# Two-layer decoder: a layer's product triple of 272, 272, 272 columns becomes 274, 270, 272

## The chip, the core and the metric

One core of a Trainium2 chip runs the whole program. The metric is the device time in microseconds, a median of three runs; a profile of one more execution shows where it goes. Engines: TensorE (PE in the profile) multiplies matrices, VectorE (DVE) and ScalarE (ACT) work element by element, GpSimd (POOL) makes masks and small copies, SyncE (SP) issues most DMAs.

## What is computed

A decoder trunk of two layers over T = 272 tokens (16 learned meta tokens and 256 of input), width 2048, 16 heads. Layer 0 has softmax attention with forget gates, layer 1 stick-breaking attention on a shared K/V. Each layer has a squared-ReLU MLP of width 8192. Only the 256 input tokens are returned, so layer 1 works on 256 columns, but K/V is made from all 272. Cut to the main line:

```python
for layer in range(DEPTH):
    a = rms_norm(h, norm_attn[layer])
    if layer < N_A_LAYERS:
        q, k, v, f_logit = split(a @ fox_w_in[i])
        o = forgetting_attention(q, k, v, cum_logf)
        h = h + o @ fox_w_o[i]
    else:
        k_s, v_s = split(rms_norm(h, kv_norm) @ w_kv)
        o = stick_breaking_attention(a @ sb_w_q[i], k_s, v_s)
        h = h + o @ sb_w_o[i]
    h = h + squared_relu_mlp(rms_norm(h, norm_mlp[layer]), w_up[layer], w_down[layer])
return rms_norm(h, final_norm)[:, N_META:]
```

## The kernel before

Activations lie feature-major: 128 features on the partitions, 16 chunks of features, and the tokens as columns (272 in layer 0, 256 in layer 1). All large products keep fp32 accuracy by splitting: an operand is the sum of a high part, rounded to the type fp32r, and a low part, the rest. A product W·x is then three products of the fast type, accumulated in the same PSUM tile: W high by x high, W high by x low, W low by x high. Such a set of three is called a triple below.

`Split` (line 121) holds the two parts of an activation in one SBUF tile, 640 columns for each chunk: in layer 0 the high part at columns 48 to 319, the low part at 368 to 639 (`ROWS`, line 27), with free columns between them. In layer 1 it also gives `wide`, the high part with six zero columns behind it. The parts are written by ACT (high) and DVE (low) in `split_chunk` (line 137), in `put_split` for attention outputs (line 456) and in the MLP's evacuation (lines 640 and 641).

`gemm_group` (line 230) makes 512 output features, four results of 128 in four PSUM tiles (`accs`). It walks over four blocks `kb` of four chunks. `weights` (line 201) fetches a block by DMA in two halves on SP's queue and splits it, high on ACT (line 225), low on DVE (line 226); there are four buffers of raw and of split weights. In the first and last block the products go result by result (12 in a row for one result), in the two others by halves of the block. Layer 0 (`t0 = 0`) takes the three products of a triple one behind the other (line 258); layer 1 takes all high-by-high products of a run first, then the others (line 256). In every fourth group of layer 1 three products take `wide` and so 262 columns. Every product is issued in `gemm_matmul` (line 190), and so has line 192 in the profile; outside the first group it also ties each product behind the one before, so that their order stands as written. A scheduler decides where the attention's own products go between them, and the order of ACT and DVE.

After the last block each result is handed to `evac`, which the caller gives: q, k and v are scaled into SBUF (lines 468 and 472), out-projections add to the residual stream and split the next input (lines 616 to 620), MLP up-projections apply ReLU, square and split (lines 633 to 642), down-projections add to the residual (line 306). Groups with 272 columns: 12 for q, k and v of layer 0, 4 for its out-projection, 32 for its MLP (four chunks `f` of 2048 hidden features, each four groups up and four down), 8 for the shared K/V; 56 in all.

Of the kernel before, what the change touches and what calls it, by code (L numbers as in the profile page):

```python
# [9 lines left out]
F32 = mybir.dt.float32  # L10
F32R = mybir.dt.float32r
AF = mybir.ActivationFunctionType
ALU = mybir.AluOpType
AX = mybir.AxisListType

P = 128
# [4 lines left out]
T = M + S  # L21
# [12 lines left out]
def yoco_kernel(ctx: ExitStack, tc: tile.TileContext, hT_in, gains, b_f, w_f, w_qkv0, w_o0, w_up, w_dn,  # L34
                w_kv, w_q1, w_o1, g_row, out):
    nc = tc.nc
# [7 lines left out]
    tmp = ctx.enter_context(tc.tile_pool(name="tmp", bufs=2))  # L44
# [76 lines left out]
    class Split:  # L121


        def __init__(self, label, t0):
            n = T - t0
            self.t0 = t0
            rows = xs.tile([P, NC * XROW + 64], F32R, tag="x", name=f"x_{label}")
            hi, lo = ROWS[t0]
            rows = rows[:, hi:hi + NC * XROW].rearrange("p (c t) -> p c t", c=NC)
            d = lo - hi  # L130
            self.hi, self.lo = rows[:, :, :n], rows[:, :, d:d + n]
            if t0:

                self.wide = rows[:, :, :n + 6]
                nc.gpsimd.tensor_copy(rows[:, :, n:n + 6], pad[:, :6].unsqueeze(1).to_broadcast([P, NC, 6]))

    def split_chunk(sp, gi, c):

        g = g_sb[:, gi, c:c + 1]
        nc.scalar.activation(sp.hi[:, c], hT[:, c, sp.t0:], AF.Copy, scale=g)  # L140
        nc.vector.scalar_tensor_tensor(out=sp.lo[:, c], in0=hT[:, c, sp.t0:], scalar=g,
                                       in1=sp.hi[:, c].bitcast(F32), op0=ALU.mult, op1=ALU.subtract)

    class Norm:

# [84 lines left out]
    def gemm_group(wblk, sp, t0, evac, before={}, after={}, load_x=None):  # L230

        uid[0] += 1
        u = uid[0]
        accs = [pacc.tile([P, 512], F32, tag="acc", name=f"acc_{u}_{m}") for m in range(4)]
        n = T - t0
        for kb in range(4):
            if kb in before:
                before[kb]()  # L240
            parts, on_act, on_dve = weights(u, kb, wblk, 16 if t0 else 0, load_x)
            if kb in after:
                with tc.issue_after(on_act.ins), tc.issue_after(on_dve.ins):
                    after[kb]()

            if load_x is not None and kb == 0:
                runs = [([kc], range(4)) for kc in range(4)]
            elif kb in (0, 3):
                runs = [(range(4), [m]) for m in range(4)]
            else:  # L250
                runs = [(range(2 * hf, 2 * hf + 2), range(4)) for hf in range(2)]
            pinned[0] = load_x is None
            for kcs, ms in runs:
                pairs = ((0, sp.hi), (0, sp.lo), (1, sp.hi))
                if t0:
                    products = [(kc, m, *pair) for pair in pairs for kc in kcs for m in ms]
                else:
                    products = [(kc, m, *pair) for m in ms for kc in kcs for pair in pairs]
                left = {m: 3 * len(kcs) for m in ms}

                wide = [(0, 0, 0), (1, 0, 1), (2, 1, 1)] if t0 and u % 4 == 1 else []
                if u == 90:

                    wide = [(0, 0, 0), (0, 0, 1), (0, 2, 1)]
                for kc, m, part, x in products:
                    first, left[m] = kb == kc == 0 and left[m] == 3 * len(kcs), left[m] - 1
                    nw = n
                    if m == (0 if u == 90 else 3) and x is sp.hi and (kb, kc, part) in wide:
                        x, nw = sp.wide, n + 6
                    gemm_matmul(accs[m][:, :nw], parts[kc // 2][part][:, kc % 2, m * P:(m + 1) * P], x[:, 4 * kb + kc],  # L270
                                start=first, stop=kb == kc == 3 and left[m] == 0)
                if kb == 3:
                    for m in ms:
                        evac(m, accs[m][:, :n])

    def token_group(wblk, sp, done):
# [135 lines left out]
    def scratch(t, products):  # L412
        for pr in range(2):
            y = t[:, pr].rearrange("p (c x) -> p c x", c=4)
            for a in range(4):
                ins = nc.scalar.dma_start(v_dram[pr].rearrange("c j a x -> a j c x")[a], y[32 * a:32 * a + 32])
                behind(ins, products[pr])
# [38 lines left out]
    def put_split(sp, h, nh, t, n, src):  # L456
        hi, lo = (x[:, h:h + nh, t - sp.t0:t - sp.t0 + n] for x in (sp.hi, sp.lo))
        nc.scalar.activation(hi, src, AF.Copy)
        nc.vector.tensor_tensor(out=lo, in0=src, in1=hi.bitcast(F32), op=ALU.subtract)

    ao = Split("o0", 0)
    for g in range(4):
# [72 lines left out]
        for pr in range(2):  # L535
# [9 lines left out]
            for a in range(4):  # L545
# [10 lines left out]
                                in0=pm[:, P - M:P].unsqueeze(1).to_broadcast([P, 8, M]))  # L556
# [32 lines left out]
        def outputs(g=g, pps=pps, vT=vT, own=own, turned=turned):  # L589
            if turned is not None:  # L590
                scratch(turned, issued[20:60:20])
                vs = values_back(turned, issued[100:120:10], issued[160:180:10], f"0_{g}")
            for pr in range(2):
                raw, p0, p1 = pps[pr]

                p0 = p0.rearrange("p x i q -> p x (i q)").rearrange("p x (a h b i) -> p x h b a i", a=4, h=2, b=2)
                p0 = [[p0[:, k, i] for i in range(2)] for k in range(2)]
                p1 = p1.rearrange("p i q -> p (i q)").rearrange("p (a h i) -> p h a i", a=4, h=2)
                v0, v1 = vs[pr] if turned is not None else token_major(vT, pr, 0, f"0_{g}_{pr}")
                po = patt.tile([P, 2, 256], F32, tag="patt", name=f"po0_{g}_{pr}")  # L600
                for i in range(2):
                    weighted(po, v0, p0, i)
                    nc.tensor.matmul(po[:, i, P:], v1[:, i, :], p1[:, i], start=False, stop=i == 1)  # L603
                ends = po.rearrange("p i (c q) -> p (i c) q", c=2)[:, :, P - M:]
                nc.vector.tensor_tensor(out=ends, in0=ends, in1=own[:, 4 * pr:4 * pr + 4], op=ALU.add)
                put_split(ao, 4 * g + 2 * pr, 2, M, S, po)

        if g == 3:
            outputs()
# [14 lines left out]
    def mlp(layer, xm, norm, t0, last_evac, last_group=None):  # L624
        box = {}

        def get_rstd():
            box["r"] = norm.finish()

        for f in range(N_FF):  # L630
            u = Split(f"u{layer}_{f}", t0)
            for g in range(4):
                def evac(m, acc, g=g):
                    c = 4 * g + m
                    r = tmp.tile([P, T], F32, tag="relu", name=f"relu_{layer}_{f}_{c}")
                    u2 = tmp.tile([P, T], F32, tag="u2", name=f"u2_{layer}_{f}_{c}")
                    nc.vector.scalar_tensor_tensor(out=r[:, t0:], in0=acc, scalar=0.0, in1=box["r"][:, t0:],
                                                   op0=ALU.max, op1=ALU.mult)
                    nc.scalar.activation(u2[:, t0:], r[:, t0:], AF.Square)
                    nc.scalar.activation(u.hi[:, c], u2[:, t0:], AF.Copy)  # L640
                    nc.vector.tensor_tensor(out=u.lo[:, c], in0=u2[:, t0:], in1=u.hi[:, c].bitcast(F32),
                                            op=ALU.subtract)
                gemm_group(w_up[layer, f, g], xm, t0, evac, {2: get_rstd} if f == g == 0 else {})
                if last_group is not None and f == N_FF - 1 and g == 0:
                    to_token_major()
            for g in range(4):
                def evac(m, acc, g=g):
                    residual_add(4 * g + m, acc, t0)
                    if f == N_FF - 1:
                        last_evac(4 * g + m)  # L650
                if last_group is not None and f == N_FF - 1 and g == 3:
                    last_group(w_dn[layer, f, g], u)
                else:
                    gemm_group(w_dn[layer, f, g], u, t0, evac)
# [32 lines left out]
    ao = Split("o1", M)  # L687
    for g in range(4):
# [12 lines left out]
        kc = packed(kT[:, :, 240:T], f"kc_{g}")  # L701
# [23 lines left out]
        for pr in range(2):  # L725
# [10 lines left out]
            if pr == 0:  # L736
# [4 lines left out]
                                    in1=maskB[:, 0:256].unsqueeze(1).to_broadcast([P, 2, 256]))  # L741
            nc.vector.tensor_tensor(out=zp[:, :, 256:400], in0=pb[:, :, :144], op=ALU.add,
                                    in1=maskB[:, 256:400].unsqueeze(1).to_broadcast([P, 2, 144]))
# [20 lines left out]
            for t in (240, 384):  # L764
                nc.vector.tensor_tensor(out=zp[:, :, t:t + M], in0=zp[:, :, t:t + M],
                                        in1=sc[:, 2 * pr:2 * pr + 2, :], op=ALU.add)
# [184 lines left out]
```

## Time and profile before

| | |
|---|---|
| median of 3 runs | 2280.68 us (2280.51 to 2281.49) |
| the profiled execution, first to last instruction | 2278.5 us |
| PE busy | 2271.1 us, 18898 products |
| weight loads (PEld) | 2262.8 us |
| DVE busy, ACT busy | 1333.5 us, 1065.1 us |
| mean granted clock of TensorE | 0.999 |

The profile has one execution only, so sums are made against its 2278.5 us; the median of the timed runs is 2.2 us above that. How to read it: "mean ns" of a product is from its start to its modelled end, and products overlap, so it is not the time by which one product puts off the next. That time is the distance between starts, and in a stretch without waits it is the length of the stretch over the number of products. The chain of waits lists such stretches as pieces with a count.

### The profile page before, as it was taken

What the parts mean: (1) busy time and instruction counts of PE and PEld (TensorE: products, weight loads), DVE (VectorE), ACT (ScalarE), POOL (GpSimd) and SP (SyncE); (2) the same over time, 40 slices, a digit from 0 to 9 for tenths busy, and PEclk for the clock granted to TensorE, in tenths of its full rate; (3) what the DMA queues carried; (4) which work ended last, traced back from release to release, by engine and by line L of the source; (5) the groups of instructions that cost most, each with busy time, mean ns of one, the idle gap of its engine ahead of it and who ended that gap; (6) DMA issues with size and microseconds to landing.
All of it is one profiled execution on the core that took longest, in us unless ns stands there. A gap on an engine that the chain in (4) does not pass through costs nothing.

```text
span 2278.5 us, 44956 instructions
## 1 busy us (share of the span) xinstructions
PE 2271.1 (100%) x18898; PEld 2262.8 (99%) x18898; DVE 1333.5 (59%) x1930; ACT 1065.1 (47%) x1471; POOL 39.4 (2%) x72
## 2 busy tenths in 40 slices
PE   9999999999999999999999999999999999999998
PEld 9999999999999999999999999999999999999998
DVE  7767566554455455455566666666555555555555
ACT  6444445443354344335445555555443544543554
POOL 1000000000000000000000000000000000000001
PEclk9999999999999999999999999999999999999999
DMA  7765665555555555555556555555656556566564
GB/s 238 228 198 188 222 184 176 181 172 180 182 176 185 167 185 179 174 185 169 186 183 193 168 174 169 167 185 190 202 187 201 192 189 201 184 200 195 186 201 141
DMA packets 146171, 425.19 MB, mean 187 GB/s; under 512 B 31648, under 2 KB 43824, under 8 KB 145968
## 3 DMA queue, kind: packets, MB, share of 16 engines
q1 hardware_dynamic: 113760, 406.29, 54.1%
q10 hardware_dynamic: 32208, 16.02, 2.6%
q8 instruction: 148, 2.42, 0.4%
q14 instruction: 55, 0.45, 0.1%
HBM read 413.85 MB, written 8.41 MB: 185 GB/s over the span
## 4 chain that ended last, share of the span: by engine, by line
PE 99%; DMA 0%; issue 0%; POOL 0%; SPq 0%; POOLq 0%; ACT 0%; DVE 0%
PE acc L192 97%; PE po L435 0%; PE ps L435 0%; PE pza L435 0%; DMA raw<-w_qkv 0%; PE pzb L735 0%; PE po L804 0%; PE ps L508 0%; PE po L603 0%; PE pf L354 0%; PE pta L757 0%; PE pta L756 0%; PE pv L394 0%; POOL ob L850 0%; PE ptb L709 0%
## 5 line engine op out<-in xcount | busy, mean ns | idle before, releaser
L226 DVE TENSOR_TENSOR wlo<-raw,whi 128x1024 fp32r<-128x1024 f32 (+1 forms) x773 | 928.5, 1216 | 715.6 <-ACT whi L225 706.6
L225 ACT ACTIVATE whi<-raw 128x1024 fp32r<-128x1024 f32 (+1 forms) x773 | 796.4, 1050 | 961.0 <-PE acc L192 913.4
L192 PE MATMUL acc<-x_m,whi 128*128 128x272 f32 (+1 forms) x4096 | 643.1, 282 | 0.0
L192 PE MATMUL acc<-x_u,whi 128*128 128x272 f32 (+1 forms) x3968 | 626.0, 282 | 0.0
L192 PEld LDWEIGHTS acc<-x_m,whi 128*128 128x128 f32 x4096 | 566.0, 188 | 0.1
L192 PEld LDWEIGHTS acc<-x_u,whi 128*128 128x128 f32 x3968 | 550.4, 188 | 0.0
L192 PE MATMUL acc<-x_m,wlo 128*128 128x272 f32 (+1 forms) x2048 | 441.4, 282 | 0.0
L192 PE MATMUL acc<-x_u,wlo 128*128 128x272 f32 (+1 forms) x1984 | 432.1, 282 | 0.0
L192 PE MATMUL acc<-x_a,whi 128*128 128x272 f32 (+1 forms) x2048 | 355.4, 286 | 0.2 <-ACT whi L225 0.2
L192 PEld LDWEIGHTS acc<-x_m,wlo 128*128 128x128 f32 x2048 | 323.5, 188 | 0.0
L192 PEld LDWEIGHTS acc<-x_u,wlo 128*128 128x128 f32 x1984 | 315.3, 188 | 0.0
L192 PEld LDWEIGHTS acc<-x_a,whi 128*128 128x128 f32 x2048 | 301.3, 189 | 1.7 <-ACT whi L225 1.1
L192 PE MATMUL acc<-x_a,wlo 128*128 128x272 f32 (+1 forms) x1024 | 253.8, 286 | 0.0
L192 PE MATMUL acc<-x_kv,whi 128*128 128x272 f32 x1024 | 191.7, 288 | 0.0
L192 PEld LDWEIGHTS acc<-x_a,wlo 128*128 128x128 f32 x1024 | 175.7, 188 | 0.7 <-DVE ssq_a L158 0.4
L192 PE MATMUL acc<-x_o,whi 128*128 128x272 f32 (+1 forms) x1024 | 163.1, 283 | 0.0
L192 PEld LDWEIGHTS acc<-x_kv,whi 128*128 128x128 f32 x1024 | 160.1, 189 | 0.1
L192 PE MATMUL acc<-x_kv,wlo 128*128 128x272 f32 x512 | 147.6, 288 | 0.0
L192 PEld LDWEIGHTS acc<-x_o,whi 128*128 128x128 f32 x1024 | 142.3, 188 | 0.0
L307 DVE TENSOR_TENSOR hT<-acc,hT 128x272 f32<-128x272 f32 (+1 forms) x156 | 67.3, 431 | 75.4 <-PE acc L192 75.2
L192 PE MATMUL acc<-x_o,wlo 128*128 128x272 f32 (+1 forms) x512 | 110.7, 282 | 0.0
L192 PEld LDWEIGHTS acc<-x_kv,wlo 128*128 128x128 f32 x512 | 96.6, 189 | 0.0
(255 smaller groups left out, 1065.5 us busy)
## 6 DMA issues: line engine op xcount, KB each, us to landing
raw<-w_up SPq DMA_DIRECT2D x256, 512.0 KB, 3.9
raw<-w_dn SPq DMA_DIRECT2D x256, 512.0 KB, 4.0
raw<-w_qkv SPq DMA_DIRECT2D x92, 512.0 KB, 4.3
raw<-w_o SPq DMA_DIRECT2D x64, 512.0 KB, 3.9
raw<-w_kv SPq DMA_DIRECT2D x64, 512.0 KB, 4.4
raw<-w_q SPq DMA_DIRECT2D x32, 512.0 KB, 4.7
p_dram<-raw_p ACTq DMA_DIRECT2D x32, 96.0 KB, 4.6
v_dram<-turned ACTq DMA_DIRECT2D x48, 64.0 KB, 3.8
```

Source lines behind the costliest of these rows:

```text
L192: ins = nc.tensor.matmul(*args, **kw).ins
L225: on_act = nc.scalar.activation(hp, src, AF.Copy)
L226: on_dve = nc.vector.tensor_tensor(out=lp, in0=src, in1=hp.bitcast(F32), op=ALU.subtract)
L307: nc.vector.tensor_tensor(out=hT[:, c, t0:], in0=acc, in1=hT[:, c, t0:], op=ALU.add)
```

## The change

For activations of 272 columns, the high part's tile gets `more` further columns (2; 4 and 6 in the second and third chunk of the MLP) right behind it, in the free space of the row. `ended` copies the last `more` columns of the low part into them. The product of high weights with the high part now covers 272 + `more` columns, so its last columns are high weights by the last low columns; the product with the low part covers only 272 - `more`; the third stays at 272. The sums in the last columns of the PSUM tile belong to the columns `more` to the left of the tile's 272nd. Before each result is handed to `evac`, ACT copies them to SBUF (`rest`) and DVE adds them in place. In the changed kernel the lines from here on stand up to 22 lines lower.

```diff
     class Split:
-        def __init__(self, label, t0):
+        def __init__(self, label, t0, more=2):
             n = T - t0
-            self.t0 = t0
+            self.t0, self.more = t0, 0 if t0 else more
...
+            else:
+                self.wide, self.end = rows[:, :, :n + more], rows[:, :, n:n + more]
+                self.short = self.lo[:, :, :n - more]
+
+        def ended(self, c, nch=1):
+
+            if self.more:
+                nc.vector.tensor_copy(self.end[:, c:c + nch], self.lo[:, c:c + nch, T - self.more:])
 
     def split_chunk(sp, gi, c):
...
+        sp.ended(c)
...
                     nw = n
-                    if m == (0 if u == 90 else 3) and x is sp.hi and (kb, kc, part) in wide:
+                    if sp.more and x is sp.lo:
+                        x, nw = sp.short, n - sp.more
+                    elif sp.more and part == 0:
+                        x, nw = sp.wide, n + sp.more
+                    elif m == (0 if u == 90 else 3) and x is sp.hi and (kb, kc, part) in wide:
                         x, nw = sp.wide, n + 6
...
                     for m in ms:
+                        if sp.more:
+                            ends = accs[m][:, n - sp.more:n]
+                            rest = tmp.tile([P, 8], F32, tag="rest", bufs=4, name=f"rest_{u}_{m}")[:, :sp.more]
+                            nc.scalar.copy(rest, accs[m][:, n:n + sp.more])
+                            nc.vector.tensor_tensor(out=ends, in0=ends, in1=rest, op=ALU.add)
                         evac(m, accs[m][:, :n])
...
                 put_split(ao, 4 * g + 2 * pr, 2, M, S, po)
+                ao.ended(4 * g + 2 * pr, 2)
...
-            u = Split(f"u{layer}_{f}", t0)
+            u = Split(f"u{layer}_{f}", t0, (2, 4, 6, 2)[f])
...
+                    u.ended(c)
```

## The prediction

> **What bounds the kernel now.** I read the page first, then the longest pieces of the chain of waits in order of time, then the PE groups with shapes kept apart, then the PE timeline at a few places.
>
> ```profile
> span 2278.5 us, 44956 instructions
> ...
> PE 2271.1 (100%) x18898; PEld 2262.8 (99%) x18898; DVE 1333.5 (59%) x1930; ACT 1065.1 (47%) x1471; POOL 39.4 (2%) x72
> ...
> PEclk9999999999999999999999999999999999999999
> ...
> PE acc L192 97%; PE po L435 0%; PE ps L435 0%; PE pza L435 0%; DMA raw<-w_qkv 0%; PE pzb L735 0%; PE po L804 0%; PE ps L508 0%; PE po L603 0%; PE pf L354 0%; PE pta L757 0%; PE pta L756 0%; PE pv L394 0%; POOL ob L850 0%; PE ptb L709 0%
> ```
>
> TensorE is busy in all of the span, its clock is granted in full, and 97% of the chain is line 192, the projection products. Nothing else decides the end. What a product costs is read from how many follow one another in a stretch without a wait, not from its "mean ns", since products overlap. The two longest pieces of the chain, start, length and what:
>
> ```profile
> 427.93 756.83 PE acc L192 x6144
> ...
> 1581.78 533.37 PE acc L192 x4704
> ```
>
> The first lies in layer 0: 756.83 / 6144 = 123.2 ns for a product of 272 columns. The second lies in layer 1: 533.37 / 4704 = 113.4 ns for 256 columns. Sixteen columns more cost 9.8 ns, or 0.61 ns each, while 113.4 / 256 is 0.44 ns each. So 272 columns pay a surcharge. The PE timeline shows its form (start, length, engine, line); these are the products with wlo, the third of each triple, in layer 0:
>
> ```profile
> 600.07 0.29 PE L192 MATMUL acc<-x_u,wlo 128*128 128x272 f32 x1
> ...
> 600.43 0.29 PE L192 MATMUL acc<-x_u,wlo 128*128 128x272 f32 x1
> ...
> 600.81 0.28 PE L192 MATMUL acc<-x_u,wlo 128*128 128x272 f32 x1
> ...
> 601.17 0.29 PE L192 MATMUL acc<-x_u,wlo 128*128 128x272 f32 x1
> ...
> 601.55 0.29 PE L192 MATMUL acc<-x_u,wlo 128*128 128x272 f32 x1
> ```
>
> The triples take 0.36, 0.38, 0.36, 0.38 us in turn: equal work, two prices, alternating. In other stretches the same triple has another price:
>
> ```profile
> 143.15 0.29 PE L192 MATMUL acc<-x_a,wlo 128*128 128x272 f32 x1
> ...
> 143.53 0.29 PE L192 MATMUL acc<-x_a,wlo 128*128 128x272 f32 x1
> ...
> 143.91 0.29 PE L192 MATMUL acc<-x_a,wlo 128*128 128x272 f32 x1
> ```
>
> Here it is 0.38 each time. In layer 1 a stretch just before a product that the kernel widens to 262 columns is dearer than the one after it:
>
> ```profile
> 1583.50 1.11 PE L192 MATMUL acc<-x_m,wlo 128*128 128x256 f32 x8
> 1584.45 1.99 PE L192 MATMUL acc<-x_m,whi 128*128 128x256 f32 x16
> ...
> 1587.18 1.07 PE L192 MATMUL acc<-x_m,whi 128*128 128x256 f32 x8
> 1588.09 0.62 PE L192 MATMUL acc<-x_m,wlo 128*128 128x256 f32 x4
> 1588.54 1.07 PE L192 MATMUL acc<-x_m,whi 128*128 128x256 f32 x8
> ```
>
> From 1583.50 eight products take 0.95 us, 119 ns each; from 1587.18 twelve take 1.36 us, 113.3 ns each. So the cost of a product is not a function of its width alone: a stream of equal products locks into one of several rhythms and keeps it until something uneven passes. That is what the change touches.
>
> **A unit for the sum.** I count in steps of 113.33 / 17 = 6.67 ns, the time that 16 columns and no surcharge would take: 256 columns are 16 blocks of 16 and cost 17 steps, blocks plus one. 272 columns are 17 blocks; plus one would be 18 steps, 120.0 ns. They cost 123.2 to 123.3, which is 18.5: 18 and 19 in turn. A triple is then 18+19+18 = 55 steps (366.7 ns) or 19+18+19 = 56 (373.3), which are the 0.36 and 0.38 of the rows; the stretch at 143 us is at 57 (380).
>
> **The change, part by part.** *Widths.* In layer 0 and in the shared K/V projection each triple of 272, 272, 272 becomes 274, 270, 272 (276, 268, 272 in MLP chunk 1, and 278, 266, 272 in chunk 2). How many:
>
> ```profile
> L192 PE MATMUL acc<-x_m,wlo 128*128 128x272 f32 x1024 | 293.9, 287 | 0.0
> ...
> L192 PE MATMUL acc<-x_u,wlo 128*128 128x272 f32 x1024 | 293.9, 287 | 0.0
> ...
> L192 PE MATMUL acc<-x_a,wlo 128*128 128x272 f32 x768 | 216.9, 289 | 0.0
> ...
> L192 PE MATMUL acc<-x_kv,wlo 128*128 128x272 f32 x512 | 147.6, 288 | 0.0
> ...
> L192 PE MATMUL acc<-x_o,wlo 128*128 128x272 f32 x256 | 73.5, 287 | 0.0
> ```
>
> One wlo product per triple: 1024 + 1024 + 768 + 512 + 256 = 3584 triples. Columns stay at 816 in each. In blocks, 274 (and 276, 278) reaches into an 18th, while 270, 268 and 266 still need 17: 18 + 17 + 17 = 52, and one step more for each product gives 55. That is the cheaper of the two prices that alternate now. I take it that the uneven triple ends the alternation, as a wider product ends the dear stretch above. Then each pair of triples saves one step: 3584 / 2 x 6.67 = 11.9 us. The trace has no stream of uneven widths, so this is a choice between ends. The low end is 54 steps, each product at 18 as if the two columns beyond the block were free: 3584 x 1.5 x 6.67 = 35.8 us saved. For this end speaks the run with a 262-column product:
>
> ```profile
> 1749.04 1.08 PE L192 MATMUL acc<-x_m,whi 128*128 128x262 f32 x8
> 1749.95 0.62 PE L192 MATMUL acc<-x_m,wlo 128*128 128x256 f32 x4
> ```
>
> Its eight products take 0.91 us, as the eight from 1587.18 without it, so six columns past the block cost no more than about 0.01 us. The high end is 56.5 steps, the extra block paid and the alternation kept: one step more per triple, 23.9 us. I take 55, between them, since it is a price that 272-column triples already show.
>
> The Trainium skill ("TensorE: Matmul & The Clock Gate", section "Back-to-back issue gap") prices a warm product in isolation at N / 2.4 + 2.5 ns, a straight line in the columns. By it a triple would be 347.5 ns with either split, and the change would be worth nothing; the trace disagrees with the figure, at 123.2 ns for 272 columns against its 115.8, and with a straight line through one stream, since one width has several prices here.
>
> *Side work.* Each of 56 groups (12 for q, k and v, 4 out-projections, 32 MLP, 8 K/V) has 4 results, so 224 tiny copies on ACT (rest) and 224 adds on DVE; and 120 copies on DVE move the end columns of the low part (ended). Nearest rows, small copies and adds out of PSUM:
>
> ```profile
> L803 ACT COPY own<-pvc 128x64 f32<-128x64 f32 x4 | 0.8, 198 | 0.0
> ...
> L805 DVE TENSOR_TENSOR po<-po,own 128x32 f32<-128x32 f32 x8 | 1.6, 195 | 2.7 <-PE po L804 2.7
> ...
> L377 DVE COPY fq_sb<-pfq 128x32 f32<-128x32 f32 x1 | 0.2, 191 | 1.5 <-PE pfq L376 1.5
> ```
>
> ACT gets 224 x 0.20 = 45 us, DVE 344 x 0.19 = 65 us. Both have room: ACT is busy 47% and DVE 59%, and their largest waits are for PE and for each other (columns: us in total, times, longest):
>
> ```profile
> ACT whi L225 <- PE acc L192: 913.4, 466, 4.6
> ...
> DVE wlo L226 <- ACT whi L225: 706.6, 419, 3.6
> ```
>
> The new waits are: on ACT the copy waits for the last product of a result, with weight splits (line 225) queued behind it, which wait for PE anyway; on DVE the add waits for that copy, with the evacuation and a weight split behind it. An accumulator is wanted again only after the three other results' runs of 12 products, 3 x 12 x 0.123 = 4.4 us, and the addition delays it by 0.4. I cost it at nothing. Were that cover gone at each group, 56 x 0.4 = 22 us would be the price.
>
> *Order.* In the built program PE has the same products, and the order on the queues of SP and POOL and of the DMAs on ACT is unchanged. In MLP and out-projection the PE order is unchanged too; in the attention stages the scheduler lets attention products slide by up to 49 places and ACT and DVE instructions change places with neighbours. There the DMA that comes back from scratch is what can come late:
>
> ```profile
> ACT v L385 <- DMA turned<-v_dram: 6.6, 6, 2.7
> ```
>
> ACT waits 6.6 us in all for it now and PE hardly waits; I take 0 for the new order, with 6.6 us either way as bounds, which lie inside the range below.
>
> *The start.* The first product of a chunk now reads the copied low columns, so it waits for the low split too.
>
> ```profile
> 4.85 0.50 DVE L141 SCALAR_TENSOR_TENSOR x_a<-hT,g_sb,x_a 128x272 fp32r<-128x272 f32 x1
> ...
> 4.98 1.16 PE L192 MATMUL acc<-x_a,whi 128*128 128x272 f32 x5
> ...
> 7.23 1.26 PE L192 MATMUL acc<-x_a,whi 128*128 128x272 f32 x8 [0.22 <-ACT whi L225]
> ```
>
> The low split ends at 5.35; with 0.19 for the copy PE begins at about 5.55 instead of 4.98. Part of that 0.6 us is taken back in the wait at 7.23: 0 to 0.6, I take 0.5.
>
> **Sum.** 2278.5 - 11.9 + 0.5 = 2267.1 us of span. The median of the runs is 2280.7, 2.2 us above this span, and I keep that: **2269.3 us**.
>
> **Rivals.** *Every product at 18 steps or nearly* (54 to 54.5 per triple): the uneven triple lets each product find the cheap rhythm that 256 columns have. For it: the cheap run after the wide product and the free six columns. Against: no stretch of 272 is that cheap. 54.5 gives 3584 x 6.67 = 23.9 saved, 2257.3; 54 gives 2245.4.
>
> *Only columns count*: the sum stays 816 and the surcharge belongs to the load of columns, not to a rhythm. Against it: three prices for one width. Time 2280.7 + 0.5 = 2281.2.
>
> *The extra block* (the slower side): 274 columns pay a further step, 270 give none back, and the alternation goes on in part or in full. It decides from where the triple averages over 55.5 steps, 370 ns. For it: longer products show larger surcharges, not a constant one.
>
> ```profile
> 2257.03 1.99 PE L192 MATMUL acc<-whi,x_u 128*128 128x512 f32 x8
> ...
> 2259.78 1.99 PE L192 MATMUL acc<-whi,x_u 128*128 128x512 f32 x8
> ```
>
> Twelve products of 512 columns take 2.75 us, 229.2 ns or 34.4 steps each, 2.4 above their 32 blocks; and the 57-step stretch shows that worse rhythms exist. At 56 steps the loss is 11.9 us, 2293.1; at 56.5 it is 23.9, 2305.1.
>
> **How the numbers follow.** Forecast (55 steps) 0.37, cheaper rhythm 0.30, columns only 0.09, extra block 0.24. The measurement can tell about 0.2% from no change, 4.6 us. So faster 0.67, same 0.09, slower 0.24. The range runs from the cheap end, 2245, to just above the 56-step case, 2294; what it leaves out is the dearer half of the extra block and the cover's loss. If faster, the likeliest part is 2245 to 2271.
>
> **What would show each step right or wrong.** The long layer-0 piece of the chain: 122.2 ns per product if right, 120 to 121 for the cheaper rhythm, 123.2 if only columns count, 124.4 or more for the extra block. The distance between wlo products on the timeline: a steady 0.37 instead of 0.36 and 0.38. Layer 1's piece must stay at 113.4. The MLP chunks, with their own widths, would differ if the overhang matters and not the unevenness. A new wait of PE on "rest" or on the copied ends beyond the first 10 us would make the side work wrong, and so would weight splits that come late behind the new copies.

## The result and the profile after

The change makes the kernel slower: 2309.2 us against 2280.6 us before, a ratio of 1.0127 (95% interval 1.0113 to 1.0141). The profiled execution spans 2306.4 us, 27.9 more than before. From the page of the changed kernel: the span, and busy time, share and instructions of each engine.

```profile
span 2306.4 us, 45617 instructions
...
PE 2296.7 (100%) x18898; PEld 2287.5 (99%) x18898; DVE 1381.4 (60%) x2274; ACT 1092.9 (47%) x1695; POOL 21.6 (1%) x72
```

TensorE has the same 18898 products as before and is busy all the time, so its products follow one another more slowly. The two long pieces of the chain of waits (start, length, what) say where:

```profile
436.19 771.25 PE acc L201 x6144
...
1609.65 533.37 PE acc L201 x4704
```

The piece in layer 1 lasts 533.37 us for 4704 products, to the hundredth what it lasted before. The piece in layer 0 has the same 6144 products as before and lasts 14.4 us longer: 125.5 ns each instead of 123.2. The timeline of PE in MLP chunk 0, the first and the 27th of a run of wlo products:

```profile
611.95 0.29 PE L201 MATMUL acc<-x_u,wlo 128*128 128x272 f32 x1
...
621.76 0.29 PE L201 MATMUL acc<-x_m,wlo 128*128 128x272 f32 x1
```

26 triples of (274, 270, 272) in 9.81 us are 377 ns per triple, 56.6 of the prediction's steps, where 370 (55.5) were paid before and 366.7 (55) were forecast.

The next table cuts all spans at the starts of products: a group is 192 products of line 192 (201 in the changed kernel), and a stage ends where the first product of the next stage's first group starts. It is worked out from the trace; times are in us, and the last stage ends with the span. (*Widths* and *side work* are the first two experiments below.) One of the ten timed executions of the side work alone had a granted clock of 0.948 and took 2316.2 us; it is in the ratio given for that run and hardly moves its median.

```
stage               before   changed   widths alone   side work alone
first group          32.64     32.86          32.86             33.39
q, k, v groups      284.22    290.07         288.11            287.46
out-projection       98.62    100.55         100.57             98.62
MLP of layer 0      758.22    772.72         773.28            758.22
q of layer 1         87.65     87.82          87.82             87.81
shared K/V          217.00    222.25         220.84            218.53
out-projection 1     91.94     91.88          91.96             91.96
MLP 1 and end       708.23    708.25         708.20            708.19
```

Nearly all that the change costs lies in the stages with 272 columns; more than half of it in the MLP of layer 0.

### The profile page after: what moved, and what is told of

It reads as the page before. It is cut to its first block, busy times and chain, and to the rows that moved or that the text cites. A ratio compares the mean times of both kernels' runs of the same rounds, so it can differ in the third digit from the quotient of the medians.

```text
span 2306.4 us, 45617 instructions
## 1 busy us (share of the span) xinstructions
PE 2296.7 (100%) x18898; PEld 2287.5 (99%) x18898; DVE 1381.4 (60%) x2274; ACT 1092.9 (47%) x1695; POOL 21.6 (1%) x72
## 4 chain that ended last, share of the span: by engine, by line
PE 96%; DVE 1%; DMA 1%; issue 0%; ACTq 0%; ACT 0%; POOL 0%; SPq 0%; POOLq 0%; DVEq 0%
PE acc L201 94%; DMA fk<-f_dram 1%; DVE wlo L235 0%; PE po L453 0%; PE pza L453 0%; ACT whi L234 0%; DMA p_dram<-raw_p 0%; DVE s L511 0%; PE ps L453 0%; ACTq L585 0%; PE po L824 0%; PE pzb L755 0%; DVE turned L427 0%; DMA hT<-hT_in 0%; PE ps L526 0%
## 5 line engine op out<-in xcount | busy, mean ns | idle before, releaser
L201 PE MATMUL acc<-x_m,whi 128*128 128x256 f32 (+2 forms) x4096 | 651.0, 282 | 0.0
L201 PE MATMUL acc<-x_u,whi 128*128 128x256 f32 (+6 forms) x3968 | 632.5, 282 | 0.0
L201 PE MATMUL acc<-x_a,whi 128*128 128x274 f32 (+2 forms) x2048 | 361.5, 287 | 1.3 <-ACT x_a L148 0.9
L201 PE MATMUL acc<-x_kv,whi 128*128 128x274 f32 (+1 forms) x1024 | 195.1, 289 | 0.4
L201 PE MATMUL acc<-x_o,whi 128*128 128x256 f32 (+2 forms) x1024 | 164.8, 283 | 0.1
L290 ACT COPY rest<-acc 128x2 f32<-128x2 f32 (+2 forms) x224 | 34.5, 154 | 132.2 <-PE acc L201 126.2
```

The costliest lines, as they stand in the source:

```text
L201: ins = nc.tensor.matmul(*args, **kw).ins
L290: nc.scalar.copy(rest, accs[m][:, n:n + sp.more])
```

## The experiments

Prices per product below are worked out from the trace: the time from the start of the 25th to the start of the last product of a group of 192, over the number between. A price times three over 6.67 ns is steps per triple. Most sweeps give each of the 32 MLP groups of layer 0 a case of its own, so that one run holds 32 measurements; their price is read from the group, and the time of the whole run says nothing by itself. The first MLP group of each run also holds two products of the norm (`pms_m`), 0.46 us in its middle, so its mean is too high by 2.8 ns. And the same case can have another price behind another group (e5), so a price that was measured once, in one group, is that of the case and of what went before.

**e1, the widths alone.** The copies and additions are taken out and the end columns hold zeros.

```diff
-            if self.more:
-                nc.vector.tensor_copy(self.end[:, c:c + nch], self.lo[:, c:c + nch, T - self.more:])
+            pass
...
-                        if sp.more:
-                            ends = accs[m][:, n - sp.more:n]
...
-                            nc.vector.tensor_tensor(out=ends, in0=ends, in1=rest, op=ALU.add)
```

> The changed kernel's widths (274, 270, 272 and so on) without the side work: the end columns hold zeros and nothing is added, so the low part of the last columns is left out. If the widths set the time (theory A: each uneven triple takes 377.8 ns instead of 370), it is as slow as the changed kernel: 2308 us, +28 over the kernel before, and a layer-0 group of 192 products lasts 24.18 us. If the side work or its waits set it (theory B), it is at 2280 or below, and the group lasts 23.7 or less.

Measured: 2306.0 us, ratio 1.0113 (1.0096 to 1.0130). The long piece of its chain:

```profile
434.25 771.81 PE acc L201 x6144
```

As long as in the changed kernel (771.25). A group of 192 products in chunk 0 lasts 24.18 us, as theory A expected. The widths alone cost 25.6 us.

**e2, the side work alone.** The copies and additions stay, all products have 272 columns.

```diff
-                    if sp.more and x is sp.lo:
-                        x, nw = sp.short, n - sp.more
-                    elif sp.more and part == 0:
-                        x, nw = sp.wide, n + sp.more
-                    elif m == (0 if u == 90 else 3) and x is sp.hi and (kb, kc, part) in wide:
+                    if m == (0 if u == 90 else 3) and x is sp.hi and (kb, kc, part) in wide:
...
-                            nc.scalar.copy(rest, accs[m][:, n:n + sp.more])
+                            nc.scalar.copy(rest, accs[m][:, n - sp.more:n])
```

> The changed kernel's copies and additions, with all products at 272 columns (the addition doubles the last columns, so those are not the reference's). Theory A (widths): within 3 us of the kernel before, 2278 to 2284 us. Theory B (side work): about 2308 us.

Measured: 2285.2 us against 2280.5 (medians), ratio 1.0034 (1.0007 to 1.0061), and

```profile
431.94 756.98 PE acc L201 x6144
```

In the long MLP piece the side work costs nothing (756.83 before). It costs 4.8 us all the same, against the expectation of at most 3, nearly all in the attention stages: in the profiled execution 3.2 in the q, k, v groups, 1.5 in K/V and 0.8 in the very first group. Theory A holds for the bulk, but the side work is not free.

**e3, one width per group.**

```diff
+WIDTHS = [256, 258, 260, 262, 264, 266, 268, 270, 272, 274, 276, ...]
+PLAN = {17 + i: (n, n, n) for i, n in enumerate(WIDTHS)}
...
+                    if u in PLAN:
+                        nw = max(n, *PLAN[u]) if first else PLAN[u][1 if x is sp.lo else 2 * part]
+                        x = (sp.row if x is sp.hi or nw > T else sp.lo)[:, :, :nw]
```

> The kernel before, where each of the 32 MLP groups of layer 0 has products of one width of its own, 240 to 320 columns, so sums over columns are left out or filled with others. Block theory: the price of a product is a whole number of 6.67 ns steps per started block of 16 columns plus a rhythm, so 274 jumps by a step or more over 272 and then stays flat up to 288, and 270 costs as much as 272. Line theory: the price rises by about 0.62 ns for each column, 274 at 124.6 and 270 at 122.1, and only the mixture of widths in a triple is dear. Alignment theory: the price depends on the width modulo 32 or 64 with minima at 256, 288 or 320.

Measured, in ns per product (two numbers: the same width in two groups):

```
240  112.2           248  116.5
256  *     113.7     268  124.4 126.6     280  128.9 126.7
258  121.0           270  124.6 124.5     282  129.3
260  120.0           272  123.3 123.3     284  133.3 133.3
262  120.1           274  126.7 126.7     286  126.7
264  120.6 120.6     276  126.7 126.7     288  133.3
266  123.3           278  128.9           296  140.0
304  138.6           320  146.7
 * first MLP group: 117.8 up to the two products of the norm, 113.3 behind them
```

Under 272 columns the first product of each result keeps 272, and what follows it can be dearer for a while: 264 columns settle at 120.0, though their mean is 120.6. Over 272 columns the second product reads the high part's row too; that by itself costs nothing, since in e8's first group, where all products of 272 columns read that row from its start, the price is 123.3 before and behind the norm's products.

The rows behind the three widths of the main triple, first and 27th wlo product of a run at 270, at 272 and at 274 columns:

```profile
583.77 0.29 PE L199 MATMUL acc<-x_u,wlo 128*128 128x270 f32 x1
...
593.48 0.29 PE L199 MATMUL acc<-x_u,wlo 128*128 128x270 f32 x1
...
608.00 0.29 PE L199 MATMUL acc<-x_m,wlo 128*128 128x272 f32 x1
...
617.62 0.29 PE L199 MATMUL acc<-x_m,wlo 128*128 128x272 f32 x1
...
631.83 0.29 PE L199 MATMUL acc<-x_m,wlo 128*128 128x274 f32 x1
...
641.72 0.29 PE L199 MATMUL acc<-x_m,wlo 128*128 128x274 f32 x1
```

26 triples take 9.71, 9.62 and 9.89 us: 272 columns are *cheaper* than 270, and 274 are 3.4 ns dearer than 272. None of the three theories holds as put. The block theory has the jump from 272 to 274, but it is half a step and not a whole one, the price is not flat after that, and 286 is cheaper than 278. The line theory fails at 270 and 286. The alignment theory fails too, since 288 is dear and 286 cheap; and 256, 268 and 280 each have two prices. What stands, for the weights where this kernel has them: 272 is a dip, and both of its neighbours, 270 and 274, cost more than it does.

**e4, triples with a sum of 816.**

```diff
+TRIPLES = [(272, 272, 272), (274, 270, 272), (276, 268, 272), (278, 266, 272), ...]
+PLAN = {17 + i: t for i, t in enumerate(TRIPLES)}
```

> The kernel before, where each of the 32 MLP groups of layer 0 has a triple of widths of its own, all with a sum of 816: (272+k, 272-k, 272) for k from 0 to 240, and for k = 2, 4, 6, 16 also with the surplus in the third product or in the second; columns are left out or filled with others. Block theory: (288, 256, 272) needs 18 + 16 + 17 = 51 blocks, one fewer than (274, 270, 272), and takes at most 370 ns per triple, while k = 2 to 14 all take 373 to 378. Mixture theory: any k over 0 is dearer than 370, k = 16 too. Line theory: all near 370. The order in the triple changes nothing in the block theory.

Measured, mean ns per product:

```
(272, 272, 272)   123.3 (126.1 in the first group, with the norm's products)
(274, 270, 272)   126.0 126.0     (272, 270, 274)  125.6     (270, 274, 272)  125.5
(276, 268, 272)   124.4           (272, 268, 276)  124.5     (268, 276, 272)  125.6
(278, 266, 272)   125.5           (272, 266, 278)  125.6     (266, 278, 272)  125.6
(280, 264, 272)   124.4           (272, 256, 288)  124.5     (256, 288, 272)  124.7
(288, 256, 272)   124.5           (304, 240, 272)  126.6     (512, 32, 272)   156.4
```

No split of the 816 columns came under 272 three times; the best uneven ones cost 56.0 steps per triple instead of 55.5. So (288, 256, 272), with one block fewer, is not the bargain of the block theory.

**e5, the order of the products.** By kind means that the high-by-high products of a run go first, then high-by-low, then low-by-high, so that neighbours have one width.

```diff
-                if t0:
+                if t0 or u in PLAN and BY_KIND[u - 17]:
                     products = [(kc, m, *pair) for pair in pairs for kc in kcs for m in ms]
```

> The kernel before; the 32 MLP groups of layer 0 take in turn the triples 272x3, (274, 270, 272), (276, 268, 272), (278, 266, 272), each in two orders: triple by triple, or by kind (4 to 16 products of one width behind one another), and each four times; end columns hold zeros. Theory 1 (each width has its own price in a stream of its own: 274 at 126.67, 270 at 124.55, 272 at 123.33): by kind, (274, 270, 272) costs the mean of these, 124.9 ns, against 125.9 triple by triple. Theory 2 (only the neighbourhood of unlike widths costs): by kind it comes down to about 123.3. Theory 3 (order plays no part): 125.9 in both.

Measured, ns per product over the repeats (the first group left out):

```
                   triple by triple      by kind
(272, 272, 272)    123.33                123.33
(274, 270, 272)    125.98                125.17
(276, 268, 272)    124.45 to 125.19      125.23 to 125.32
(278, 266, 272)    125.51 to 126.67      125.37 to 125.40
```

Theory 1 comes nearest: by kind, (274, 270, 272) costs 125.17, close to the mean of the three prices of e3, (126.67 + 124.55 + 123.33) / 3 = 124.85. So of the 2.65 ns that this triple costs over 272, 1.84 remain when unlike widths meet only where one kind gives way to the next; 0.81 belongs to the closer mixture. What went before counts as well: (276, 268, 272) triple by triple costs 125.19 behind a group of (274, 270, 272) and 124.45 behind a group of its own widths, twice each.

**e6, the place of the weights.** The split weights are shifted in their buffers, nothing else.

```diff
-            parts, on_act, on_dve = weights(u, kb, wblk, 16 if t0 else 0, load_x)
+            parts, on_act, on_dve = weights(u, kb, wblk, 16 if t0 else OFFSETS[u - 17] if u in PLAN else 0, load_x)
```

> The kernel before; the split weights of the 32 MLP groups of layer 0 lie 0, 2, 4, ... 62 columns further in their buffers; all products have 272 columns and the result is the reference's. Theory 1 (the rhythm comes from where the weight columns and the token columns lie relative to each other, so that the two reads meet): the price per product varies with the offset, with a period of 16 or 64 columns, from 120 to 130 ns. Theory 2 (the rhythm comes from the length of the product alone): 123.3 ns at every offset.

Measured for 272 columns, ns per product by the shift in columns:

```
 0 126.1*  8 123.3   16 126.7   24 125.3   32 126.7   40 125.7   48 125.3   56 126.7
 2 123.3  10 126.7   18 126.7   26 126.7   34 125.9   42 124.4   50 125.9   58 126.7
 4 126.7  12 126.7   20 126.7   28 126.7   36 125.7   44 126.7   52 126.7   60 124.4
 6 124.5  14 123.4   22 127.8   30 123.4   38 126.7   46 126.7   54 124.4   62 123.3
 * first group, with the norm's two products in it; 123.3 in its second half, and in all later MLP groups of the kernel before, which have offset 0
```

The price moves with the place of the weights, from 123.3 to 127.8, with no plain period. Theory 1 holds in that, theory 2 falls. Each place was measured once, behind a group at another place, so how much of a single price is the place and how much the entry is not shown; at shift 0 the kernel before has 126.7 as well, in the stretch at 143 us. No place gives less than 123.3, and only six of the 32 give that.

**e7, single uneven products.**

```diff
+                        nw = max(n, n + KICKS[u - 17]) if first else PLAN[u][1 if x is sp.lo else 2 * part]
+                        if x is sp.hi and part == 0 and kb in (1, 2) and (kc, m) in ((0, 2), (2, 2)):
+                            nw += KICKS[u - 17]
```

> The kernel before; in each of the 32 MLP groups of layer 0 four products of 192 are wider or narrower than 272 by an amount of the group's own (0, 2 to 32, 40 to 240, and -2 to -128); columns beyond 272 are never used, the narrower ones leave sums out. If 272 columns have a cheaper rhythm that a single uneven product can reach and that then lasts (as 256 columns do), some groups fall to 120.0 ns for part of their 192 products; if 123.33 is the best rhythm of 272, none does, and some rise to 126.7.

With a positive amount the first product of each of the four results is wider too.

Measured: groups with products wider by 2 to 6 columns cost 123.57 on average, by 8 to 32 mostly 123.8 to 124.1 (125.6 at 18), by 240 columns 127.2; narrower by 2 to 128 columns 123.2 to 124.5. Over any 12 products of 272 columns between two uneven ones the price is 123.25 at the least; a few products behind an uneven one it is back at 123.33 nearly everywhere, but three groups (18, -4 and -128) have stretches at 126.67. No group shows 120.0 for a part. The 123.33 of 272 columns is the best rhythm that any run here reached; no push made it better, and some made it worse.

**e8, the place of the tokens.**

```diff
+STARTS = [(0, 0), (2, 0), (4, 0), ..., (48, 0), (4, 4), (8, 8), (12, 12), (16, 16), (24, 24), (32, 32), (48, 48)]
...
+                        x = sp.row[:, :, STARTS[u - 17][0]:STARTS[u - 17][0] + nw]
```

> The kernel before; in the 32 MLP groups of layer 0 all products read 272 columns of the high part's row from 0, 2, ... 48 columns further right, and in the last seven groups the weights are shifted by the same amount as well (4, 8, 12, 16, 24, 32, 48); the sums are not the reference's. If the place of weights relative to tokens sets the rhythm, the prices are those of the weight offsets with the sign turned, and equal shifts of both change nothing (123.3 ns). If the absolute place of the token columns sets it, equal shifts change the price as the token shift alone does. If neither matters, 123.3 everywhere.

Measured: with the tokens shifted alone, 123.3 (at 44) to 128.0 (at 42), and 126.6 to 126.7 at 13 of the 24 shifts. With tokens and weights shifted by the same amount, 123.32 to 123.34 in six of seven cases, and 126.65 for (12, 12). That points to the place of the weight columns relative to the token columns, with one case against it. The prices are not simply those of e6 with the sign turned; that each group also takes over a rhythm from the one before would explain it, but was not tested here.

**e9, the small copy on DVE.**

```diff
-                            nc.scalar.copy(rest, accs[m][:, n - sp.more:n])
+                            nc.vector.tensor_copy(rest, accs[m][:, n - sp.more:n])
```

> As the side work alone with all products at 272 columns, but the small copy (rest) is made by DVE instead of ACT. Theory Q (the 4.8 us of the side work alone come from the copies in ACT's queue, which put off the DMAs and weight splits behind them in the attention stages): within 1.5 us of the kernel before, and no PE gap over 0.4 us in the attention stages. Theory L (the longer way from product to evacuation, or the many DVE instructions, cost it): about 2285 again.

Measured: ratio 1.0023 (1.0014 to 1.0033), 2286.3 against 2280.5 us. Theory Q falls: without copies in ACT's queue the side work costs as much.

**e10, the uneven triple at other places.** The edit is that of e6 with the triple (274, 270, 272) in each group.

> The triple (274, 270, 272) in all 32 MLP groups of layer 0, with the weights 0, 2, 4, ... 62 columns further in their buffers; the end columns hold zeros. If the loss belongs to the uneven triple itself, no offset brings it under 123.33 ns per product; if it belongs only to the place that was tuned for 272 columns, some offset brings it to 122.2 (55 steps per triple) or below.

Measured: 124.40 (shift 60) to 128.86 (34 and 54), 127.28 or less at 29 of 32 shifts. No place brings the triple under 123.33, though several are better than the changed kernel's: 124.4 to 124.5 at shifts 18, 36, 40, 60, 62. By the expectation that would say that the loss belongs to the uneven triple. But e6 has no place under 123.33 for 272 columns either, so that bound does not tell the two apart. Shift by shift, without the first group, the uneven triple is dearer than 272 three times at 12 places, cheaper at 12 and within 0.3 ns at 7; the means are 126.05 and 125.68. So uneven triples are hardly dearer on average over these places. As far as the two sweeps show, what the change loses is for the most part that 272 columns had one of their few good places in the kernel before, and the uneven triple does not profit from it.

**e11, the changed kernel by kind.** The small copy is on DVE here, too.

```diff
-                if t0:
+                if t0 or load_x is None:
...
-                            nc.scalar.copy(rest, accs[m][:, n:n + sp.more])
+                            nc.vector.tensor_copy(rest, accs[m][:, n:n + sp.more])
```

> The whole changed kernel, with the products of a run ordered by kind (products of one width behind one another, as layer 1 does) and the small copy on DVE. From the sweeps: 125.2 to 125.4 ns per product instead of 125.9, so 20 us of widths and nothing for the side work: 2299 to 2302 us, slower than the kernel before by 0.85% and faster than the changed kernel by 8 us. If only the neighbourhood of unlike widths cost, it would be at 2281 to 2284.

Measured: 2305.7 us, ratio 1.0109 (1.0094 to 1.0125). The price of its products in the MLP is as expected, 125.17 to 125.41 ns by groups; the long piece of its chain:

```profile
436.38 768.11 PE acc L201 x6144
```

The whole is 3.7 us above the range expected. In the first out-projection group PE stands still once for 2.1 us, for the copied ends of `x_o` (waits of PE: us in total, times, longest),

```profile
PE acc L201 <- DVE x_o L143: 2.1, 1, 2.1
```

and the K/V stage lasts 222.8 us, against 217.0 before; there the chain shows waits for the scratch transfers, such as

```profile
1337.47 5.03 DMA v_dram<-turned
1344.48 5.54 DMA v_dram<-turned
1350.12 3.29 DMA turned<-v_dram
```

No version tried beats the kernel before.

**e12, the copied ends alone.**

```diff
-                        if sp.more:
+                        if False:
                             ends = accs[m][:, n - sp.more:n]
```

> All products at 272 columns, and of the side work only the 120 copies of the low part's last columns; the small copy and the addition before each evacuation are left out, and nothing uses the copied columns. If the addition before the evacuation (later kT, vT and what the scheduler makes of it) costs the side work's 5 us, this is within 1.5 us of the kernel before, 2279 to 2282, and the attention stages last 284.2 and 217.0 us as before. If the copied ends cost it, about 2285.

Measured: ratio 1.0019 (1.0010 to 1.0028), 2285.6 against 2280.8 us. The q, k, v groups last 289.8 us instead of 284.2, the K/V stage 217.0 as before. So the copied ends alone are enough to cost about 5 us in the first attention stage; the 1.5 us in K/V of e2 come with the small copies and additions. The chain of e12 in the first attention stage names a transfer through scratch,

```profile
82.22 5.02 DMA p_dram<-raw_p
87.94 3.91 DMA p<-p_dram
94.93 3.39 PE acc L201 x18
```

where that of the kernel before has products only:

```profile
81.79 7.91 PE acc L192 x64
```

The timeline of ACT shows what waits. In the kernel before, the round trip is issued like this (ACTq are the DMAs that ACT issues; L567 reads back),

```profile
77.52 2.15 ACTq L546 DMA_DIRECT2D p_dram<-raw_p  x4
81.09 0.59 ACTq L567 DMA_DIRECT2D raw_p<-p_dram  x1
81.73 0.77 ACTq L567 DMA_DIRECT2D p<-p_dram  x1
82.54 1.06 ACT L225 ACTIVATE whi<-raw 128x1024 fp32r<-128x1024 f32 x1 [4.71 <-DMA p_dram<-raw_p]
```

and in e12 like this:

```profile
84.32 2.01 ACTq L560 DMA_DIRECT2D p_dram<-raw_p  x4
87.31 0.59 ACTq L581 DMA_DIRECT2D raw_p<-p_dram  x1
87.94 0.68 ACTq L581 DMA_DIRECT2D p<-p_dram  x1
...
91.84 0.21 ACT L571 COPY pm_sb<-pm 128x64 f32<-128x64 f32 x1 [7.60 <-DMA p<-p_dram]
...
92.57 1.06 ACT L234 ACTIVATE whi<-raw 128x1024 fp32r<-128x1024 f32 x1 [0.51 <-issue]
```

The last write of the scratch is issued some 7 us later, and ACT stands still for 7.60 instead of 4.71 us. The weight split at 92.57 is the 53rd of the program; in the kernel before the 53rd starts at 86.37. PE waits for it and for DVE's half:

```profile
93.67 0.52 PE L201 MATMUL acc<-x_a,whi 128*128 128x272 f32 x2 [1.67 <-ACT whi L234]
94.93 0.39 PE L201 MATMUL acc<-x_a,wlo 128*128 128x272 f32 x1 [0.74 <-DVE wlo L235]
```

Just behind this pause something follows that costs time as well: the granted clock of TensorE falls from 1.00 to 0.50 for 3.41 us, from 96.23 on. In this view of a stretch the number before the last two is the granted clock (in front of it the length of the stretch and the busy time of PE, PEld, DVE, ACT and POOL, behind it DMA):

```profile
96.20:99.60 3.40, 3.40 (x17) 3.40 (x17) 2.82 (x4) 2.13 (x4) 0.00 (x0) 0.51 0.87 308
```

By an estimate from the clock alone, half of these 3.41 us is lost, 1.7 of e12's 5. The profile of e9 has the same, from 97.18, also for 3.41 us and behind a pause of 2.8 us; e2, with pauses of 1.1 and 0.7 us, and the changed kernel, with one of 0.7, have no such stretch there. So e2, e9 and e12 cost about the same, but not in the same way. What they share is a wait of PE between 92 and 98 us that the kernel before and e1 do not have.

## Why the prediction was wrong, point by point

- **What bounds the kernel** was right: TensorE's stream of projection products sets the time; layer 1's MLP did not move by 0.1 us, and 25.6 of the 28.6 us lost come from products that follow one another more slowly (e1).
- **The step that failed** is the choice of 55 steps per triple: "That is the cheaper of the two prices that alternate now", and with it "I take it that the uneven triple ends the alternation". There is no such pair of prices. The distances of 0.36 and 0.38 us were read from starts rounded to 0.01; from the unrounded starts of the same rows, triples last 368 to 372 ns, 369 and 371 on average in turn, not 366.7 and 373.3. In e3 the same triple lasts 0.37 on average, 9.62 us for 26. 55.5 is one rhythm's price, and e6, e7 and e8 found none cheaper for 272 columns: 123.33 ns is the lowest price that any run reached for them, not a mean of a cheap and a dear one. In place of 55 steps the changed triples cost 56.6, 377 ns; so the uneven triple ended the best rhythm of 272 columns, and not a dear one.
- **The price of the uneven triple** was counted as blocks plus one. Measured in streams of their own, with the weights where this kernel has them, 274 costs 57 steps per triple, 270 costs 56, 272 costs 55.5 (e3). The two columns that move cost 3.4 ns where they arrive, and give nothing back where they leave: 270 is 1.2 ns dearer than 272. These prices make 1.5 of the 2.7 ns that a product loses by the mean of e3, 1.8 by e5; the rest is the mixture. Over 3584 triples, 7.8 ns each would be 28.0 us; 25.6 were lost, since some groups pay less, such as (276, 268, 272) at 125.2 in e1 (124.4 in the changed kernel). Only the down-projections of chunks 1 and 2 have the wider splits, and their groups, at 124.4 and 125.5 ns, are cheaper than the 125.9 of (274, 270, 272): a larger overhang did not cost more. The prediction had no term for the place of weights and tokens: at other places 272 columns cost up to 127.8 (e6), and there the uneven triple is often the cheaper one (e10).
- **The rival that came true** is the extra block, at 56.7 steps instead of the 56 or 56.5 that it was priced at, with a chance of 0.24. Its reason was only part of it: a further block for 274 without one less for 270. The other part, that 270 is dearer than 272 by itself, was in no rival. The 57-step stretch, quoted as a worse rhythm, was the better hint: 274 and 276 columns stay at exactly that price.
- **The free six columns** were a wrong witness. That a single wider product in a stream of 256 costs next to nothing does not say what a stream with a wider product in every triple costs. Nor does a wider product only end dear stretches: in e3's second group of 256 columns, the product of 272 at the start of a result is followed by some six distances of up to 123 ns before they are back at 113.
- **Only columns count** is refuted in e3, where 286 columns cost 126.7 ns and 284 cost 133.3. The straight line that the Trainium skill ("TensorE: Matmul & The Clock Gate", section "Back-to-back issue gap") gives for a product in isolation does not hold for this stream either.
- **The side work at nothing** was right in the MLP and the out-projections (756.98 against 756.83 us in e2) and wrong in the attention stages: 4.8 us. The cover named there was DVE's and ACT's idle share over the whole span; in the first attention stage it is not there. In the changed kernel PE waits there once for 0.7 us (a weight split), and twice, 0.4 us together, where the profile names a copy of ends on DVE as what ended the wait, the kind of wait that the prediction called a sign against it. The bound given for the new order, 6.6 us, holds the loss.
- **The start** was to cost 0.5 us. PE begins at 6.19 and not at the 5.55 forecast, 1.2 us later than before; yet the first group ends at 32.86 instead of 32.64. The forecast that part is taken back was right; the 0.2 is no clean measure, since e1, without the copies, ends that group at 32.86 too.
- **The range** ended at 2294, since it took the loss to be at most the 56-step case; the 56.5-step case that was priced at 2305.1 lay outside.

What stays open: why the relative place of weight and token columns gives just these prices, why 272 and 286 are dips, and how much of each price in a sweep is the case and how much what went before it. That two reads meet would fit e6 and e8, but no run here shows it. Nor is it settled which of the small instructions moves the first attention stage's transfers, since e2, e9 and e12 cost about the same with different ones, and e9 and e12 lose part of it to the halved clock. Why the clock was halved there and not in e2 no run here settles.

## What to carry to other kernels

Where TensorE is the bound, the price of a product is not a function that one can interpolate: measure the very stream, with its widths, its order and its places in memory, before summing thousands of it. A stream that has been tuned by placement can sit in a dip; here, moving two columns out of it cost on both sides, even though the sum of columns is the same. And before blaming the new form, measure the old one at the new form's places, too: over 31 places here the two differ by 0.4 ns on average, where at the kernel's own place it is 2.7. And before calling two distances in a timeline two prices, check that their difference is larger than the rounding of the rows.

## What the runs showed of the hardware that was not expected

- The price of a product has several values for one width: 256 columns at 117.8 or 113.3 ns, 280 at 128.9 or 126.7, at one place of weights and tokens; the groups differ in the products that went before (e3).
- It is not monotonic in the width: 286 columns cost 126.7 ns, less than 278 (128.9) and the same as 274.
- Shifting the weights by two to six columns in their buffer moves it between 123.3 and 126.7 ns at an equal width (e6); with weights and tokens shifted together it is 123.3 in six of seven cases (e8).
- In the changed kernel's stream of (274, 270, 272) the products do not settle to one distance: over a cycle of nine, the distances run from 120.0 to 130.7 ns, and together last 170 steps.
- A pause of PE can cost more than its own length: in the profiles of e12 and e9 the granted clock is 0.50 for 3.41 us just behind pauses of 2.4 us (1.67 and 0.74) and 2.8 us; behind the shorter ones of e2 and of the changed kernel, and behind one of 2.1 us in e11, it stays at 1.00.
